# A third raw weight buffer, and all small weight parts on VectorE, in a hybrid decoder layer

## The chip, the cores and the metric

The kernel runs on one core of a Trainium2 chip. The metric is device time in microseconds (us) of one execution; the kernel before was timed three times. TensorE (PE) multiplies, VectorE (DVE), ScalarE (ACT) and GpSimd (POOL) work elementwise, and SyncE (SP) issues most transfers. SBUF is the memory on the core in which all operands stand; PSUM receives the products.

## The reference

One layer of a decoder for 256 tokens of width 1024, in float32. Cut to what matters:

```python
xn = rmsnorm(h, norm_mix_g[l])
q_a, k_a, v_a, q_b, f_b, i_b, og_b, g_a, g_b = split_cols(xn @ w_in[l])   # nine 1024-wide projections
y_a = moba_attention(q_a, k_a, v_a, positions) @ w_br_attn[l]             # rotary, causal softmax, 16 heads
y_b = hgrn2(q_b, f_b, i_b, og_b, lb_all[l], hgrn_norm_g[l]) @ w_br_hgrn[l] # gated linear recurrence, 8 heads
h = h + (sigmoid(g_a) * y_a + sigmoid(g_b) * y_b) @ w_out[l]
h = h + memory_cross_attention(rmsnorm(h, norm_x_g[l]), rmsnorm(mem, norm_mem_g[l]),
                               wq_x[l], wkv_x[l], wo_x[l])                # 4 heads, 256 memory tokens
gu = rmsnorm(h, norm_ffn_g[l]) @ w_ffn_in[l]
h = h + (silu(gu[..., :2816]) * gu[..., 2816:]) @ w_ffn_out[l]
return rmsnorm(h, final_norm_g)
```

With 256 tokens there is one attention block, so each query attends its own block alone.

## The kernel before, in words

**Weight chunks.** All weights are laid out beforehand as chunks of 128 x 2048 float32 (1 MB), in the order of `plan()`. The first 64 chunks, 0 to 63, belong to everything ahead of the feed-forward part: 0 to 3 the forget gate, 4 to 7 the recurrence's query, 8 to 27 the other projections, 28 to 35 the two merge gates, 36 to 47 the branch and output matrices, 48 to 63 the cross-attention. Chunk 60 to 63 are `wo_x`. For float32 accuracy each chunk is split into a large part `hi` (rounded by ScalarE, L210) and a small part `lo` = raw - hi (L214), and a product is made of three multiplications: hi by hi, hi by lo, lo by hi (L275 to L277).

**`prep()`** does one chunk: SyncE loads it into a raw buffer (L202, L204 or L208), ScalarE makes `hi` in two halves of 1024 columns, and VectorE makes `lo`. For chunks 9 to 41 (`SHARED`) each half of `lo` is divided: VectorE takes 576 columns and GpSimd 448 (`POOL_COLS` / 2). The raw buffers are two (pool `wr`), the buffers of `hi` and `lo` three each (`wh`, `wl`). Chunk 1 has a raw buffer of its own under the tag B14; chunks 62 and 63 have their parts (`hix`, `lox`) under the tags B10, B11 and B12, B6. `nxt()` hands the next chunk to a multiplication and first calls `prep()` for all chunks up to two ahead (`LEAD`), so when TensorE begins with chunk i, chunk i+2 may be split, into the buffer that chunk i-1 leaves.

**Order.** TensorE's instructions run in the order in which the code writes them. Side work (the recurrence `hgrn`, the attention `duo`, the scores of the cross-attention) is cut into steps that `tick()` runs between multiplications. For the other engines a planner, which has its own estimate of costs, orders the instructions; each engine, and SyncE's queue of transfers, then runs in that order, and an instruction that waits holds up all behind it on its engine. In the feed-forward part the order on all engines is written by hand.

**Big buffers.** `big(tag, ...)` gives buffers that are used again under their tag, each use waiting for the last readers of the one before. The ones that matter here: B0 holds `H`, the residual, which is loaded from the token-major input `xtok` at the start, squared for the first norm (L560, into `junk` under P1) and added to from L961 and L963 on. P0 holds `QK`, the recurrence's queries and keys. B6 is 16 KB a partition: first `QQ` (16 x 256 a partition; the moving operands of the pair products, L609 and L654), then in turn `oal`, `qxl`, `lox`, and in the feed-forward part `hids`, four slots of hidden activations.

**The cross-attention's end.** `scores(x)` makes the softmax of one head: the row maximum and product on VectorE (L1046), the exponential on ScalarE (L1050), the scaling on VectorE (L1054); TensorE then transposes it (L1060, tile `xT`) and `pv` multiplies it by the values (L270 to L272). Chunks 62 and 63 are prepared about there.

**Sums for the feed-forward part.** `block_sums()` adds pairs of weight chunks in device memory by accumulating transfers, issued by ScalarE (L228, L232) and GpSimd (L234) one by one as chunks are consumed.

Of the kernel before, what the change touches and what calls it, by code (L numbers as in the profile page):

```python
# [10 lines left out]
F32 = mybir.dt.float32  # L11
F32R = mybir.dt.float32r
I32 = mybir.dt.int32
AF = mybir.ActivationFunctionType
ALU = mybir.AluOpType
# [9 lines left out]
EPS = 1e-6  # L25
NEG = -1e30
LEAD = 2
POOL_COLS = 896
SHARED = range(9, 42)
TOKENS = ((0, 1), (1, 2), (2, 4), (4, 8))  # L30
WARM = 15
PIECES = (4, 2, 2)

D1, D2, D3, D4 = 6434.0, -0.01824188232421875, -3.5660341382026672e-06, 2.549093241608853e-10
C1, C2, C3 = 6.28125, 0.0019354820251464844, -1.748455600074497e-07
# [98 lines left out]
def build(tc, A, out):  # L134
    nc = tc.nc
    V, SC, G, PE, SY = nc.vector, nc.scalar, nc.gpsimd, nc.tensor, nc.sync
    with ExitStack() as ctx:
# [11 lines left out]
        def big(tag, name, shape=(128, 8, 256), dt=F32):  # L149
            return bp.tile(list(shape), dt, name=name, tag=tag)  # L150
# [21 lines left out]
        ifq, posi = gv[:, 56:88], gv[:, 88:90].bitcast(I32)  # L172
        nhalf = cp.tile([128, 4], F32, name="nhalf")
        ident = cst[:, C_ID:C_ID + 128]
        H = big("B0", "H", (128, 2, 1024))
        ones = cp.tile([128, 1], F32, name="ones")
        V.memset(nhalf, -0.5)
        V.memset(ones, 1.0)
# [5 lines left out]
        def prep(tags=None, raw=None):  # L184
            i = made[0]
            made[0] += 1
            first = i < 2
            if raw is None:
                raw = wr.tile([128, 2048], F32, name="raw", tag="raw")
            assert i in HEAD  # L190
            if tags is None:
                hi = wh.tile([128, 2048], F32R, name="hi", tag="hi")
                lo = wl.tile([128, 2048], F32R, name="lo", tag="lo")
            else:
                hi = big(tags[0], "hix", (128, 2048), F32R)
                lo = big(tags[1], "lox", (128, 2048), F32R)
            pieces = 4 if first else 2
            n = 2048 // pieces
            sent = PIECES[i] if i < len(PIECES) else 1
            for c in range(sent if 0 < i < len(PIECES) else 0):  # L200
                a = slice(c * 2048 // sent, (c + 1) * 2048 // sent)
                SY.dma_start(raw[:, a], piece(A["w"][i], a))  # L202
            if sent == 1:
                SY.dma_start(raw, A["w"][i])  # L204
            for c in range(pieces):
                a = slice(c * n, (c + 1) * n)
                if i == 0:
                    SY.dma_start(raw[:, a], piece(A["w"][i], a))  # L208
                    yield
                SC.activation(hi[:, a], raw[:, a], AF.Copy)  # L210
                cut = (c + 1) * n - (POOL_COLS // pieces if i in SHARED else 0)
                for eng, b in ((V, slice(c * n, cut)), (G, slice(cut, (c + 1) * n))):
                    if b.start < b.stop:
                        eng.tensor_tensor(lo[:, b], raw[:, b], hi[:, b].bitcast(F32), op=ALU.subtract)  # L214
            ready[i] = (hi, lo)

        def run(g):
# [83 lines left out]
        def gemm_t(X, evict, between=()):  # L301
            between = list(between)
            pss = [mm.tile([128, 512], F32, name="pst", tag="mm") for _ in range(2)]
            for kh in range(2):
                w = by_k(nxt(), 4)
                for t in range(2):
                    t_part(pss[t], w, X, t, kh)
                    if between:
                        between.pop(0)()
                    if kh == 1:  # L310
                        evict(t, pss[t])
                tick()
# [9 lines left out]
        def rstd_of(ssq, name, n=2, mult=1.0 / D, eps=EPS):  # L322
            v = small("v_", [n])
            V.tensor_scalar(v, ssq, mult, eps, op0=ALU.mult, op1=ALU.add)
            r = cp.tile([128, n], F32, name="r_" + name)
            G.tensor_tensor(r, v, nhalf[:, :n], op=ALU.pow)
            return r
# [142 lines left out]


        fT = big("B4", "fT", (128, 16, 128))
        QK = big("P0", "QK", (128, 2, 16, 128))
        QP, KS = QK[:, 0], QK[:, 1]
        QQ = big("B6", "QQ", (128, 16, 256))

        gate_a = cp.tile([128, 8], F32, name="gate_a")
        gate_b = cp.tile([128, 8], F32, name="gate_b")
# [38 lines left out]
        def ev_q(c):  # L517
            th = {}

            def use(h0, bk):  # L520
                a = slice(2 * h0, 2 * h0 + 4)
                q4 = bk.rearrange(v4, a=2)
                V.tensor_tensor(QP[:, a], q4, fT[:, a], op=ALU.mult)
                SC.activation(QQ[:, a].rearrange("p a (w j) -> p a w j", w=4)[:, :, 0:4:3],
                              q4.rearrange("p a (j w) -> p a w j", w=2), AF.Copy)

            def ev(t, ps):
                th[t] = t2("qth")
                SC.activation(th[t], ps, AF.Silu, scale=r_x[:, t:t + 1])
                if t == 1:  # L530
                    turned(th, c, use)
            return ev
# [4 lines left out]
        run(prep())  # L537
        SY.dma_start(cst, A["cst"])
        run(prep())
        SY.dma_start(H, A["xtok"])  # L540
        SY.dma_start(lm, A["lm"])
        pss = [[mm.tile([128, 512], F32, name="psg", tag="mm") for _ in range(2)] for _ in range(2)]
        for i in range(9):
            if i < 8:
                c, k = i // 4, i % 4
# [9 lines left out]
        for t in range(2):  # L555
            t_part(pss[0][t], w, X, t, 1)
        ssqx = small("ssqx", [2])
        junk = big("P1", "junk", (128, 2, 1024))
        for t in range(2):
            SC.activation(junk[:, t], H[:, t], AF.Square, accum_out=ssqx[:, t:t + 1])  # L560
        r_x = rstd_of(ssqx, "x")
        next(rt)
        next(rt)
        r_half = cp.tile([128, 2], F32, name="r_half")
# [39 lines left out]
        def level_one(g, bs):  # L604
            for b in bs:
                a0 = 8 * g + 2 * b
                ps = bank("l1", (128, 2, 64))
                for j in range(2):
                    PE.matmul(ps[:, j], KS[:, a0 + j], QQ[:, a0 + j, 0:64], start=True, stop=True)  # L609
                V.tensor_tensor(by_parity(a0, 0), ps, bc(ident2[:, :, 0], 2, 1), op=ALU.mult)  # L610

        def widen(g, L, parts="qkt"):
# [23 lines left out]
        def pair_queries(g, L):  # L636
            ga = slice(8 * g, 8 * g + 8)
            n = 32 // L
            mv = [QQ[:, ga, 64 * i:64 * i + 64] for i in range(3)]
            SC.activation(mv[0].rearrange("p a (i j) -> p a i j", j=L), blocks(QP[:, ga], L)[1], AF.Copy)  # L640
            widen(g, L, "qt")
            wide = blocks(QP[:, ga], 2 * L)[1]
            SC.activation(mv[1].rearrange("p a (i j) -> p a i j", j=2 * L), wide, AF.Copy)
            near = tview(L, g).rearrange("p a (i w) -> p a i w", w=4)[:, :, :, 1]
            V.tensor_tensor(mv[2].rearrange("p a (i j) -> p a i j", j=2 * L), wide,
                            near.unsqueeze(3).to_broadcast([128, 8, n, 2 * L]), op=ALU.mult)

        def pair_levels(g, L, bs):
            for b in bs:
                a0 = 8 * g + 2 * b  # L650
                n = 256 if L == 2 else 192
                ps = bank("lp", (128, 2, n))
                for j in range(2):
                    PE.matmul(ps[:, j], KS[:, a0 + j], QQ[:, a0 + j, 0:n], start=True, stop=True)  # L654
                if L == 2:
                    V.tensor_tensor(by_parity(a0, 1), ps[:, :, 192:256], bc(two_rows, 2, 1), op=ALU.mult)
                for i in range(3):
                    M = L if i == 0 else 2 * L
                    li = (1 if L == 2 else 4) + i
                    mask = lm[:, 64 * li:64 * li + 64].rearrange("p (i j) -> p i j", j=M)  # L660
                    V.copy_predicated(blocks(at3[:, a0:a0 + 2], M)[1], bc(mask, 2, 1),
                                      ps[:, :, 64 * i:64 * i + 64].rearrange("p a (i j) -> p a i j", j=M))
# [219 lines left out]
        def ev_g(dst, c):  # L882
            def ev(t, ps):
                SC.activation(dst[:, t, c * 512:(c + 1) * 512], ps, AF.Tanh, scale=r_half[:, t:t + 1])
            return ev
# [23 lines left out]
        turns = []  # L909
        for c in range(2):  # L910
            gemm_t(X, ev_g(tbt, c))
        tat = big("B7", "tat", (128, 2, 1024))
        for c in range(2):
            gemm_t(X, ev_g(tat, c))
# [275 lines left out]
        raws += spare + [big("B12", "raw", (128, 2048))]  # L1190
        fetch(4)
        fetch(5)
        hids = big("B6", "hids", (128, 4, 2, 2, 256), F32R)
        Sh = big("P1", "Sh", (128, 2, 4, 4, 128), F32R)
        ts = {}

# [40 lines left out]
        def turn_hid(o):  # L1237
            bk = four[1].rearrange("p (a b) -> p a b", a=2)
            for t in range(2):
                u = hm.pop((o, t))  # L1240
                for j in range(2):
                    PE.transpose(bk[:, j, t * 128:(t + 1) * 128], u[:, j * 128:(j + 1) * 128], ident)
            hd = hids[:, o % 4]
            hid[o] = hd

            def post():
                split(bk, hd[:, 0], hd[:, 1])
            return post
# [37 lines left out]
        for k, u in enumerate(FFN[:-2]):  # L1286
# [17 lines left out]
            w = use(k)  # L1304
# [155 lines left out]
```

## Time and profile before

| | |
|---|---|
| Time, median of 3 | 624.73 us (623.67 to 625.43) |
| The profiled execution's own time | 626.06 us |
| Its span, first to last instruction | 624.3 us |
| Busy: TensorE / VectorE / ScalarE / GpSimd | 606.2 / 450.5 / 369.2 / 210.2 us |
| Mean granted TensorE clock | 0.991 of full speed |

In the profile's rows `L214` is line 214 of the kernel, `lo<-raw,hi` the tiles written and read, `x66` the count, then the summed busy time in us and the mean of one in ns; behind it the engine's idle time ahead of these instructions and what ended it. In an answer in order of time the first two columns are the start and the length in us, and a bracket holds how long the engine had been idle and what released it. Rows of windows give start:end, the length, then for TensorE, its weight loads, VectorE, ScalarE and GpSimd the busy time with the count of instructions, then the granted clock, the share of time in which the DMA engines were busy, and GB/s. Rows of DMA issues end with KB and the median us from issue to landing.

### The profile page before, as it was taken

To read this page: it belongs to the slowest core of one execution; us is meant where nothing else is said; L and a number is where in the kernel's file an instruction comes from. 1 tells how busy PE (TensorE), PEld (TensorE's weight loads), DVE (VectorE), ACT (ScalarE), POOL (GpSimd) and SP (SyncE) were. 2 spreads that over 40 slices of the span, in tenths; PEclk is the share of its full clock that TensorE was granted. 3 is DMA by queue.
4 is the path that set the end of the run, shared out by engine and by line. 5 is a ranking of instruction groups with operands and counts; after the bars stand their busy time and mean duration, and the time that the engine had idled before them with its cause. 6 is when DMAs were issued, how large, how long until landed. Compare 5 with 4: busy or idle time off the path is not lost.

```text
span 624.3 us, 8396 instructions
## 1 busy us (share of the span) xinstructions
PE 606.2 (97%) x3075; PEld 503.1 (81%) x3075; DVE 450.5 (72%) x729; ACT 369.2 (59%) x583; POOL 210.2 (34%) x202
## 2 busy tenths in 40 slices
PE   8999999999999999999999999959999999999995
PEld 7888888888877887778888888858888888888884
DVE  7556678987776775747966557746789878787863
ACT  7775454334267666745546557555477767676752
POOL 3887844665464565343302433100000000000003
PEclk9999999999999999999999999979999999999998
DMA  9775898636875656797798887765699989896601
GB/s 342 289 276 210 266 318 262 228 140 198 270 208 204 257 152 198 276 322 265 228 286 240 304 283 239 229 256 203 264 289 356 307 333 288 319 319 227 195 1 67
DMA packets 21689, 154.70 MB, mean 248 GB/s; under 512 B 2720, under 2 KB 3360, under 8 KB 5280
## 3 DMA queue, kind: packets, MB, share of 16 engines
q1 hardware_dynamic: 17568, 116.63, 49.4%
q0 software_dynamic: 2880, 20.97, 17.4%
q10 hardware_dynamic: 1200, 16.57, 7.0%
q8 instruction: 24, 0.39, 0.2%
q14 instruction: 17, 0.14, 0.1%
HBM read 153.11 MB, written 32.51 MB: 297 GB/s over the span
## 4 chain that ended last, share of the span: by engine, by line
PE 78%; DMA 9%; DVE 8%; ACT 2%; issue 1%; POOL 0%; POOLq 0%; ACTq 0%; DVEq 0%; SPq 0%
PE pst L275 10%; PE pst L277 10%; PE pst L276 10%; DMA raw<-w 8%; PE bk L275 6%; PE bk L277 6%; PE bk L276 6%; DVE lo L214 4%; PE psf L290 3%; PE acc L275 3%; PE acc L277 3%; PE acc L276 3%; PE lp L654 2%; PE psf L291 2%; ACT hi L210 1%
## 5 line engine op out<-in xcount | busy, mean ns | idle before, releaser
L214 DVE TENSOR_TENSOR lo<-raw,hi 128x576 fp32r<-128x576 f32 (+2 forms) x128 | 143.7, 1137 | 68.4 <-ACT hi L210 67.4
L210 ACT ACTIVATE hi<-raw 128x1024 fp32r<-128x1024 f32 (+1 forms) x128 | 128.0, 1028 | 109.1 <-DMA raw<-w 53.6
L214 POOL TENSOR_TENSOR lo<-raw,hi 128x448 fp32r<-128x448 f32 x66 | 98.0, 1504 | 79.2 <-ACT hi L210 72.9
L275 PE MATMUL pst<-hi,Xh 128*128 128x512 f32 x256 | 103.2, 403 | 0.0
L277 PE MATMUL pst<-hi,Xl 128*128 128x512 f32 x256 | 99.9, 390 | 0.0
L276 PE MATMUL pst<-lo,Xh 128*128 128x512 f32 x256 | 99.7, 390 | 0.0
L1165 DVE TENSOR_TENSOR lo<-raw,hi 128x1024 fp32r<-128x1024 f32 x56 | 65.9, 1218 | 13.0 <-ACT hi L1164 12.8
L1164 ACT ACTIVATE hi<-raw 128x1024 fp32r<-128x1024 f32 x56 | 56.2, 1053 | 19.8 <-issue 10.5
L277 PEld LDWEIGHTS pst<-hi,Xl 128*128 128x128 f32 x256 | 48.0, 188 | 10.3
L275 PEld LDWEIGHTS pst<-hi,Xh 128*128 128x128 f32 x256 | 48.1, 188 | 10.0 <-issue 0.7
L276 PEld LDWEIGHTS pst<-lo,Xh 128*128 128x128 f32 x256 | 48.2, 188 | 9.2
L1147 POOL DMA_DIRECT2D raw<-w x5 | 4.5, 891 | 119.2 <-DVE lo L1165 29.7
L275 PE MATMUL acc<-hi,hids 128*128 128x512 f32 x64 | 25.1, 392 | 0.0
L277 PE MATMUL acc<-hi,hids 128*128 128x512 f32 x64 | 24.9, 390 | 0.0
L276 PE MATMUL acc<-lo,hids 128*128 128x512 f32 x64 | 24.9, 389 | 0.0
L275 PE MATMUL bk<-hi,Sh 128*128 128x512 f32 x60 | 23.7, 396 | 0.0
L275 PE MATMUL bk<-hi,h2h 128*128 128x512 f32 x60 | 23.7, 394 | 0.0
L277 PE MATMUL bk<-hi,h2l 128*128 128x512 f32 x60 | 23.4, 390 | 0.0
L277 PE MATMUL bk<-hi,Sh 128*128 128x512 f32 x60 | 23.4, 390 | 0.0
L276 PE MATMUL bk<-lo,h2h 128*128 128x512 f32 x60 | 23.4, 389 | 0.0
L276 PE MATMUL bk<-lo,Sh 128*128 128x512 f32 x60 | 23.3, 389 | 0.0
L290 PE MATMUL psf<-H,hi 128*128 128x512 f32 x64 | 22.8, 400 | 0.0
(388 smaller groups left out, 1446.8 us busy)
## 6 DMA issues: line engine op xcount, KB each, us to landing
raw<-w SPq DMA_DIRECT2D x78, 1024.0 KB, 6.4
sum<-w POOLq DMA_DIRECT2D x15, 1024.0 KB, 9.8
raw<-sum SPq DMA_DIRECT2D x13, 1024.0 KB, 6.9
raws<-w SPq DMA_DIRECT2D x11, 1024.0 KB, 6.7
raw<-w POOLq DMA_DIRECT2D x5, 1024.0 KB, 8.7
raw<-w SPq DMA_DIRECT2D x4, 512.0 KB, 6.1
raws<-sum SPq DMA_DIRECT2D x2, 1024.0 KB, 6.3
raw<-w SPq DMA_DIRECT2D x4, 256.0 KB, 4.5
```

What stands on the lines that cost most here:

```text
L210: SC.activation(hi[:, a], raw[:, a], AF.Copy)
L214: eng.tensor_tensor(lo[:, b], raw[:, b], hi[:, b].bitcast(F32), op=ALU.subtract)
L275: PE.matmul(ps, xh, h, start=first, stop=False, skip_group_check=more)
L276: PE.matmul(ps, xh, l, start=False, stop=False, skip_group_check=more)
L277: PE.matmul(ps, xl, h, start=False, stop=last, skip_group_check=more)
L290: PE.matmul(ps, w[0][:, k, a], X2[:, :, k], start=k == 0, stop=False)
L291: PE.matmul(ps[:, 0], w[1][:, k, a], X2[:, 0, k], start=False, stop=k == 7)
L654: PE.matmul(ps[:, j], KS[:, a0 + j], QQ[:, a0 + j, 0:n], start=True, stop=True)
L1147: G.dma_start(raw_of[k], A["w"][AT_CHUNK["I", PAIRS[g][0], 1]], accum_op=ALU.add)
L1164: SC.activation(hi[:, a], raw[:, a], AF.Copy)
L1165: V.tensor_tensor(lo[:, a], raw[:, a], hi[:, a].bitcast(F32), op=ALU.subtract)
```

## The change

Four edits. (1) `prep()` gives every third chunk (2, 5, 8, ...) a raw buffer outside the pool of two: under B0 for chunks below 32, under a new tag B6b from then on. (2) GpSimd's share of the small parts is gone; VectorE makes each half whole. (3) To free B0, the token-major input is loaded into P0 at the start as `xtok`, where it is squared in place, and loaded again into B0 as `H` behind the first merge gate's multiplications; `QK` is allocated under P0 behind the squares. (4) To have B6b, B6's 16 KB become two tags of 8 KB: `QQ` and `hids` are each a list of two halves.

```diff
-POOL_COLS = 896
-SHARED = range(9, 42)
+THIRD = 32
...
-        H = big("B0", "H", (128, 2, 1024))
...
-            if raw is None:
+            if raw is None and i % 3 == 2:
+                raw = big("B0" if i < THIRD else "B6b", "raw", (128, 2048))
+            elif raw is None:
                 raw = wr.tile([128, 2048], F32, name="raw", tag="raw")
...
                 SC.activation(hi[:, a], raw[:, a], AF.Copy)
-                cut = (c + 1) * n - (POOL_COLS // pieces if i in SHARED else 0)
-                for eng, b in ((V, slice(c * n, cut)), (G, slice(cut, (c + 1) * n))):
-                    if b.start < b.stop:
-                        eng.tensor_tensor(lo[:, b], raw[:, b], hi[:, b].bitcast(F32), op=ALU.subtract)
+                V.tensor_tensor(lo[:, a], raw[:, a], hi[:, a].bitcast(F32), op=ALU.subtract)
...
-        QK = big("P0", "QK", (128, 2, 16, 128))
-        QP, KS = QK[:, 0], QK[:, 1]
-        QQ = big("B6", "QQ", (128, 16, 256))
+        xtok = big("P0", "xtok", (128, 2, 1024))
+        QQ = [big(tag, "QQ", (128, 8, 256)) for tag in ("B6", "B6b")]
...
-        SY.dma_start(H, A["xtok"])
+        SY.dma_start(xtok, A["xtok"])
...
-        junk = big("P1", "junk", (128, 2, 1024))
         for t in range(2):
-            SC.activation(junk[:, t], H[:, t], AF.Square, accum_out=ssqx[:, t:t + 1])
+            SC.activation(xtok[:, t], xtok[:, t], AF.Square, accum_out=ssqx[:, t:t + 1])
         r_x = rstd_of(ssqx, "x")
+        QK = big("P0", "QK", (128, 2, 16, 128))
+        QP, KS = QK[:, 0], QK[:, 1]
...
-                    PE.matmul(ps[:, j], KS[:, a0 + j], QQ[:, a0 + j, 0:n], start=True, stop=True)
+                    PE.matmul(ps[:, j], KS[:, a0 + j], QQ[g][:, a0 + j - 8 * g, 0:n], start=True, stop=True)
...
             gemm_t(X, ev_g(tbt, c))
+        H = big("B0", "H", (128, 2, 1024))
+        SY.dma_start(H, A["xtok"])
         tat = big("B7", "tat", (128, 2, 1024))
...
-        hids = big("B6", "hids", (128, 4, 2, 2, 256), F32R)
+        hids = [big(tag, "hids", (128, 2, 2, 2, 256), F32R) for tag in ("B6", "B6b")]
...
-            hd = hids[:, o % 4]
+            hd = hids[o % 4 // 2][:, o % 2]
```

More of the change, by code (lines that the diff above doesn't have):

```diff
@@ L523, in use @@
                 V.tensor_tensor(QP[:, a], q4, fT[:, a], op=ALU.mult)
-                SC.activation(QQ[:, a].rearrange("p a (w j) -> p a w j", w=4)[:, :, 0:4:3],
+                qa = slice(a.start % 8, a.start % 8 + 4)
+                SC.activation(QQ[a.start // 8][:, qa].rearrange("p a (w j) -> p a w j", w=4)[:, :, 0:4:3],
                               q4.rearrange("p a (j w) -> p a w j", w=2), AF.Copy)
@@ L608, in level_one @@
                 for j in range(2):
-                    PE.matmul(ps[:, j], KS[:, a0 + j], QQ[:, a0 + j, 0:64], start=True, stop=True)
+                    PE.matmul(ps[:, j], KS[:, a0 + j], QQ[g][:, a0 + j - 8 * g, 0:64], start=True, stop=True)
                 V.tensor_tensor(by_parity(a0, 0), ps, bc(ident2[:, :, 0], 2, 1), op=ALU.mult)
@@ L638, in pair_queries @@
             n = 32 // L
-            mv = [QQ[:, ga, 64 * i:64 * i + 64] for i in range(3)]
+            mv = [QQ[g][:, :, 64 * i:64 * i + 64] for i in range(3)]
             SC.activation(mv[0].rearrange("p a (i j) -> p a i j", j=L), blocks(QP[:, ga], L)[1], AF.Copy)
```

## The prediction

> **What bounds the kernel now.** I read the page's engine table first, then who TensorE waited for, then the windows around those waits, then the instructions there.
>
> ```profile
> span 624.3 us, 8396 instructions
> PE 606.2 (97%) x3075; PEld 503.1 (81%) x3075; DVE 450.5 (72%) x729; ACT 369.2 (59%) x583; POOL 210.2 (34%) x202
> ```
>
> TensorE is busy for 606.2 of 624.3 us, and the change issues the same matmuls. So nothing can be won except in the 18 us in which TensorE stands still. Part of that is the start and the tail, where no weight chunk of the kind in question is awaited. The rest is in this answer on TensorE's waits (columns: sum, times, longest):
>
> ```profile
> PE xT L1060 <- DVE xp L1054: 6.3, 1, 6.3
> PE aT L829 <- DVE ap L821: 1.7, 3, 0.9
> PE xs L277 <- POOL qxl L1017: 0.8, 1, 0.8
> PE as L805 <- ACT pT L831: 0.5, 1, 0.5
> PE mT L903 <- POOL tat L898: 0.3, 1, 0.3
> ```
>
> Those five sum to 9.6 us. None of them is a wait for a weight part; all are for softmax or projection steps that travel through ScalarE and VectorE. The reader should ask what held these engines. The largest wait has a second cost, seen in the windows (start:end, then busy time per engine, granted clock, DMA share and GB/s):
>
> ```profile
> 110.00:115.00 5.00, 5.00 (x26) 4.36 (x25) 4.97 (x9) 2.64 (x3) 2.44 (x2) 1.00 0.00 0
> 410.00:415.00 5.00, 0.41 (x2) 0.33 (x3) 3.24 (x6) 4.10 (x8) 0.00 (x0) 0.67 0.23 95
> 415.00:420.00 5.00, 5.00 (x31) 5.00 (x31) 2.57 (x5) 2.24 (x4) 0.00 (x0) 0.65 0.90 344
> ```
>
> After the long gap the granted clock is 0.65 to 0.67; everywhere else in the body it is 1.00. The first row shows the other half of the story: from 110 to 115 us the DMA engines move nothing, because both raw buffers are full and wait to be split, and the transfer for the next chunk starts late.
>
> **Why the long wait exists.** On ScalarE, around it:
>
> ```profile
> 403.13 0.57 ACT L316 ACTIVATE ph<-xT 128x512 fp32r<-128x512 f32 x1
> 409.79 2.00 ACT L210 ACTIVATE hix<-raw 128x1024 fp32r<-128x1024 f32 x2 [6.08 <-DMA raw<-w]
> ```
>
> The large part of chunk 62 (tile hix) stands ahead of the last softmax's exponential in ScalarE's queue and waits 6.08 us for its transfer. Queued behind it are the exponentials, then VectorE's reciprocal and scaling, then TensorE's transpose xT. The transfer was late for want of a buffer:
>
> ```profile
> 391.28 0.33 SPq L204 DMA_DIRECT2D raw<-w  x1
> 399.91 0.33 SPq L204 DMA_DIRECT2D raw<-w  x1
> ```
> ```profile
> 389.99 1.22 DVE L214 TENSOR_TENSOR lo<-raw,hi 128x1024 fp32r<-128x1024 f32 x1
> 404.81 1.22 DVE L214 TENSOR_TENSOR lo<-raw,hi 128x1024 fp32r<-128x1024 f32 x1
> ```
> ```profile
> 399.91 9.79 DMA raw<-w
> 411.79 1.18 ACT xp L1050 x4
> ```
>
> Chunk 61's transfer left at 391.28, as VectorE finished chunk 59 (389.99 + 1.22 = 391.21). Chunk 62's left at 399.91, after chunk 60, and took 9.79 us.
>
> **Part 1: the third raw buffer.** After the change chunk 62 (62 % 3 = 2) uses the buffer that chunk 59 left. So it can leave at about 391.2 instead of 399.9, which is 8.7 us earlier, and with the same 9.79 us it lands at 401.0. ScalarE then starts hix right behind ph, at 403.13 + 0.57 = 403.7, and ends at 405.7 (2.00). The exponentials end 1.18 later, at 406.9. I assume that the planner keeps the order on both engines. On VectorE the second half of chunk 61 ends at 404.81 + 1.22 = 406.0; that one does not move, as its large part waits for TensorE to give back a weight buffer. Behind it come two halves of chunk 62 and the scaling:
>
> ```profile
> 413.07 1.20 DVE L214 TENSOR_TENSOR lox<-raw,hix 128x1024 fp32r<-128x1024 f32 x1
> 414.19 0.61 DVE L1054 TENSOR_SCALAR xp<-xp,xsum 128x256 f32<-128x256 f32 x2
> ```
> ```profile
> 407.88 0.39 PE L277 MATMUL pst<-hi,M 128*128 128x512 f32 x1
> 414.60 1.16 PE L1060 MATMUL xT<-cst,xp 128*128 128x128 f32 x4 [6.33 <-DVE xp L1054]
> 415.41 0.56 PE L270 MATMUL xo<-ph,vxh 128*128 128x256 f32 x1
> 418.53 0.28 PE L272 MATMUL xo<-ph,vxl 128*128 128x256 f32 x1
> 418.65 0.28 PE L270 MATMUL xo<-ph,vxh 128*128 128x256 f32 x1
> ```
>
> 406.0 + 2 x 1.20 + 0.61, with some 0.2 for the reciprocal, is 409.2. TensorE is ready at 407.88 + 0.39 = 408.3, so about 0.9 us of 6.33 stays: a gain of 5.4. With a gap of 0.9 us the clock should hold. The 14 matmuls from 415.41 to 418.53 took 3.12 us; at the later spacing (418.53 to 418.65, 0.12) they take 1.68: 1.4 us more. Bounds for this place: 0 (it stays whole) and 6.3 + 1.4 = 7.7 (exponential first).
>
> By the Trainium skill's page "TensorE: Matmul & The Clock Gate", section "HAM oscillation — how this bites in real kernels", the clock falls only after gaps above some 3.4 us. The two windows above agree for 6.33 us; by that rule the 1.4 us come back whenever less than 3.4 us remain, as summed.
>
> The three aT waits (1.7 us) have the same form:
>
> ```profile
> 179.40 2.01 ACT L210 ACTIVATE hi<-raw 128x1024 fp32r<-128x1024 f32 x2 [1.64 <-DMA raw<-w]
> 187.83 1.06 ACT L210 ACTIVATE hi<-raw 128x1024 fp32r<-128x1024 f32 x1 [3.24 <-DMA raw<-w]
> ```
>
> ScalarE stood 1.64 and 3.24 us for a transfer, in front of exponentials or copies that the transposes need. Each is longer than TensorE's own wait behind it (0.9 at most), and one buffer's lead is a whole chunk, so I take the full 1.7; bounds 0 and 1.7. The other waits (xs, as, mT: 1.6) go through GpSimd, a projection or a buffer held by the multiplication, and I leave them; bounds 0 and 1.6. What is late next is the raw buffer no longer but the large-part buffer, of which there are still three, given back by TensorE.
>
> **Part 2: all small parts on VectorE.** GpSimd loses 66 halves, VectorE's 66 grow from 576 to 1024 columns.
>
> ```profile
> L214 POOL TENSOR_TENSOR lo<-raw,hi 128x448 fp32r<-128x448 f32 x66 | 98.0, 1504 | 79.2 <-ACT hi L210 72.9 <-DVE lo L214 2.6 <-DVE ATS L656 1.9
> L214 DVE TENSOR_TENSOR lo<-raw,hi 128x576 fp32r<-128x576 f32 x66 | 69.3, 1059 | 33.2 <-ACT hi L210 32.6 <-issue 0.5
> L1165 DVE TENSOR_TENSOR lo<-raw,hi 128x1024 fp32r<-128x1024 f32 x56 | 65.9, 1218 | 13.0 <-ACT hi L1164 12.8
> L214 DVE TENSOR_TENSOR lo<-raw,hi 128x1024 fp32r<-128x1024 f32 x1 | 1.6, 1631 | 0.0
> L623 DVE TENSOR_TENSOR QK<-QK,Tt 128x512 f32<-128x512 f32 x10 | 12.2, 1220 | 0.0
> L623 DVE TENSOR_TENSOR QK<-QK,fT 128x512 f32<-128x512 f32 x2 | 1.4, 709 | 0.0
> ```
>
> A full half costs 1.218 us where GpSimd is quiet (the feed-forward row) and 1.631 in the one case in the busy stretch. Low bound: 66 x (1.218 - 1.059) = +10.5 us of VectorE. High bound: 66 x (1.631 - 1.059) = +37.8. I take the low one: the last two rows are the same operation, 1.220 us beside GpSimd and 0.709 away from it, so VectorE is being stretched by GpSimd now, and ten of these alone give back 5.1 us. Less work than 10.5 us net is spread over 240 us, and each small part is whole 1.2 us after its large part, not after GpSimd's 1.5. On TensorE's path: 0.
>
> The Trainium skill's page "SBUF — State Buffer", section "SBUF: two separate sides", says that a VectorE operation with two SBUF inputs and a GpSimd operation that reads SBUF exclude each other for the whole instruction. By that rule the relief is real, and with GpSimd's 98 us gone it is larger than the one group I summed.
>
> What hides the longer VectorE work is the lead of two chunks. Where that cover is thin, the stage rows say so:
>
> ```profile
> 95.00:137.00 42.00, 42.00 (x201) 35.86 (x200) 37.72 (x78) 16.29 (x20) 25.03 (x17) 1.00 0.66 226
> 180.00:262.00 82.00, 79.84 (x450) 62.31 (x449) 56.22 (x161) 56.98 (x127) 41.47 (x32) 1.00 0.67 218
> ```
> ```profile
> L214 DVE TENSOR_TENSOR lo<-raw,hi 128x576 fp32r<-128x576 f32 x13 | 14.0, 1081 | 0.0
> L214 DVE TENSOR_TENSOR lo<-raw,hi 128x576 fp32r<-128x576 f32 x21 | 20.4, 974 | 12.8 <-ACT hi L210 12.2 <-issue 0.5
> ```
>
> From 95 to 137 us VectorE is busy 37.72 of 42, with 13 halves (first group); from 180 to 262 it is 56.22 of 82, with 21 halves.
>
> **Part 3: input twice, buffers split.** The second load is one more transfer of 1 MB.
>
> ```profile
> H<-xtok SPq DMA_DIRECT2D x1, 1024.0 KB, 9.0
> ```
>
> It is issued past the middle of the projections, some 90 us before the residual sum reads it, in a stage with a DMA share of 0.67; it costs SyncE's queue one issue of 0.3 us. Cost 0; if its buffer were still held, the raw transfers behind it on that queue would wait, at most one 9.0 us landing, which two buffered chunks cover. At the opening, chunk 3 no longer waits for a buffer and chunk 4 may overtake the first load:
>
> ```profile
> 25.68 1.25 ACT L512 ACTIVATE fth<-psg,r_half 128x512 f32<-128x512 f32 x2
> 27.68 0.60 PE L490 MATMUL fT__411<-cst,fth 128*128 128x128 f32 x4
> ```
>
> The transposes at 27.68 need the first of these two activations, done at 26.3: a slack of 1.4 us. A chunk of 1 MB ahead of the load could cost as much as the load takes to land, 9.0 us, so the bounds are 0 and 7.6. I take 0, because chunk 3 is ahead of the load today too and would now leave earlier. The split query and hidden buffers issue the same instructions: 0.
>
> **Sum.** 5.4 + 1.4 + 1.7 = 8.5 us. The profiled execution took 626.06 us (624.3 of span and 1.8 around it), so 617.6 there. It lay 1.3 above the median of three, 624.73; against the median that is 616.2.
>
> **Rivals.** (a) *The long wait moves.* If the planner puts chunk 63's large part before the exponential too, ScalarE waits for that transfer, which leaves only after chunk 60 (399.9) and lands near 409.7 again. For it: the planner already misjudged this one. Against: program order has it later. Then only the 1.7 us remain: 623.0, or 621 where the transfer is quicker.
> (b) *VectorE becomes the bound.* If small parts cost 1.631, the stretch from 95 to 137 gets 13 x (1.631 - 1.081) = 7.2 us into 4.3 idle, so 2.9 come out. From 180 to 262, 21 x (1.631 - 0.974) = 13.8 us stand in the queue between the softmax steps, and the aT waits grow. All of it through, with the cross-attention gain of 6.8 kept, is 624.7 + 2.9 + 13.8 - 6.8 = 634.6. It decides once more than 6.8 of the 16.7 reach TensorE. Against: the 1.220 and 0.709 above.
> (c) *The third buffer buys nothing*, because large-part buffers gate the split anyway and the order on ScalarE puts other waits at the same places: 624.7. Against: 6.08 us of waiting was for the transfer, by name.
>
> **Numbers.** The forecast has 0.62, (a) 0.18, (b) 0.10, (c) 0.10. A measurement here can tell some 0.3%, 1.9 us. Faster: 0.62 and most of (a), 0.73; the same: the rest of (a) and nearly all of (c), 0.16; slower: (b) and a trace of (c), 0.11. Low end: all 9.6 us and the 1.4 gone, 613.7, less 0.7 of spread between runs: 613.0. High end: through (a) to (c), 624.5. The forecast's own range is 613.0 to 619.
>
> **What would show it.** Right: no wait of TensorE above 1.5 us at the last xT, no window below clock 1.00 near 410, no ScalarE wait of 6 us for a raw transfer, aT waits near 0, small parts at 1.22, the QK products near 0.71, DMA without empty windows up to 300 us, VectorE busy within 5 us of 450.5. Wrong: xT still late behind a transfer (a); small parts at 1.6 and new TensorE waits between 95 and 262 us (b); ScalarE's transfer waits gone but the span unmoved (c); TensorE idle at 27 us would be the opening.

## The result and the profile after

The changed kernel takes 614.42 us (median of 4, 614.12 to 615.0); the kernel before, on the same chip, 624.34 us (median of 4). The ratio is 0.9841 with a 95% interval of 0.9823 to 0.9858. The forecast was 616.2 us. The profiled execution went from 626.06 to 614.53 us, 11.5 us; against the median it is 9.9, as the profiled execution of before lay 1.7 above its median here.

The page of the changed kernel begins so (span, then busy time and share of each engine):

```profile
span 612.7 us, 8280 instructions
PE 603.5 (98%) x3075; PEld 501.3 (82%) x3075; DVE 445.3 (73%) x729; ACT 369.3 (60%) x583; POOL 116.9 (19%) x136
```

TensorE stands still for 612.7 - 603.5 = 9.2 us, where it was 18.1, and its busy time is 2.7 us less for the same matmuls. TensorE's waits, beside the start, show which standstills are left (sum, times, longest):

```profile
PE as L803 <- ACT pT L829: 0.5, 1, 0.5
PE mT L901 <- POOL tat L896: 0.2, 1, 0.2
PE xT L1060 <- DVE xp L1054: 0.2, 1, 0.2
```

The wait at xT is 0.2 us instead of 6.3, and aT and xs have left the list. To see what each place was worth altogether, and not only its named wait, take instructions that both traces have and look how far the changed kernel is ahead at each. From the timeline of TensorE, changed kernel:

```profile
174.72 1.03 PE L787 MATMUL rT<-cst,ra 128*128 128x128 f32 x8
298.48 0.49 PE L901 MATMUL mT<-cst,tat 128*128 128x128 f32 x3
374.82 0.28 PE L272 MATMUL xs<-kxh,qxh 128*128 128x256 f32 x1
376.14 0.28 PE L274 MATMUL xs<-kxh,qxl 128*128 128x256 f32 x1
404.50 0.81 PE L1060 MATMUL xT<-cst,xp 128*128 128x128 f32 x4 [0.21 <-DVE xp L1054]
419.29 0.38 PE L1110 MATMUL h2T<-cst,H 128*128 128x128 f32 x2
```

The same instructions in the kernel before (its xT row, 414.60, stands in the prediction):

```profile
174.84 1.03 PE L789 MATMUL rT<-cst,ra 128*128 128x128 f32 x8
301.20 0.49 PE L903 MATMUL mT<-cst,tat 128*128 128x128 f32 x3
377.58 0.28 PE L275 MATMUL xs<-kxh,qxh 128*128 128x256 f32 x1
380.06 0.28 PE L277 MATMUL xs<-kxh,qxl 128*128 128x256 f32 x1
430.80 0.38 PE L1110 MATMUL h2T<-cst,H 128*128 128x128 f32 x2
```

The leads are 0.12, 2.72, 2.76, 3.92, 10.10 and 11.51 us, and 11.6 at the end of the span. So 2.6 us were won between rT and mT, where the aT transposes lie; 1.2 inside one block of twelve xs matmuls; 6.2 up to the last xT; 1.4 behind it, in the stretch whose clock was 0.65; and next to nothing elsewhere.

The windows of the changed kernel that answer to those of before (granted clock third from the end, then DMA share and GB/s):

```profile
110.00:115.00 5.00, 5.00 (x26) 4.35 (x25) 5.00 (x11) 2.64 (x3) 0.83 (x1) 1.00 0.18 26
405.00:410.00 5.00, 5.00 (x44) 5.00 (x43) 3.83 (x5) 4.82 (x7) 0.00 (x0) 1.00 0.99 403
...
95.00:137.00 42.00, 42.00 (x200) 35.85 (x200) 35.84 (x78) 16.07 (x19) 7.67 (x6) 1.00 0.86 254
```

The clock stays at 1.00 behind the last softmax. From 95 to 137 us VectorE is busy 35.84 us where it was 37.72, although it now makes all small parts there.

Around the last softmax the order is what the prediction described, a little better. SyncE's queue, then VectorE, then ScalarE, changed kernel:

```profile
387.27 0.33 SPq L204 DMA_DIRECT2D raw<-w  x1
```
```profile
385.98 1.22 DVE L211 TENSOR_TENSOR lo<-raw,hi 128x1024 fp32r<-128x1024 f32 x1
...
399.96 1.22 DVE L211 TENSOR_TENSOR lo<-raw,hi 128x1024 fp32r<-128x1024 f32 x1
```
```profile
398.95 1.04 ACT L210 ACTIVATE hix<-raw 128x1024 fp32r<-128x1024 f32 x1
...
401.35 0.60 ACT L1050 ACTIVATE xp<-xp,xmx,r 128x256 f32<-128x256 f32 x1
405.15 2.01 ACT L210 ACTIVATE hix<-raw 128x1024 fp32r<-128x1024 f32 x2 [1.95 <-DMA raw<-w]
```

Chunk 62's transfer leaves at 387.27, as chunk 59's last small part ends (385.98 + 1.22 = 387.20). Its large part finds the data there: no wait in brackets at 398.95. Chunk 63's does wait for its transfer, 1.95 us at 405.15, but behind the exponentials, where nothing of TensorE's next work stands.

ScalarE's waits, before:

```profile
ACT hi L210 <- DMA raw<-w: 53.6, 21, 11.8
ACT hi L210 <- PE pst L277: 43.7, 16, 4.7
```

and after:

```profile
ACT hi L210 <- PE pst L274: 72.8, 23, 4.7
...
ACT hi L210 <- DMA raw<-w: 1.5, 2, 1.3
```

53.6 us of waiting for transfers became 1.5. Part of that time did not vanish: the wait for TensorE, which gives back the large-part buffers, grew by 29 us. It is the next limit of the supply. TensorE's own list names a large part once, for 0.2 us, so it costs TensorE next to nothing so far.

### The profile page after: what moved, and what is told of

Read it like the earlier page. It is cut to its first block, busy times and chain, and to the rows that moved or that the text cites. A ratio compares the mean times of both kernels' runs of the same rounds, so it can differ in the third digit from the quotient of the medians.

```text
span 612.7 us, 8280 instructions
## 1 busy us (share of the span) xinstructions
PE 603.5 (98%) x3075; PEld 501.3 (82%) x3075; DVE 445.3 (73%) x729; ACT 369.3 (60%) x583; POOL 116.9 (19%) x136
## 4 chain that ended last, share of the span: by engine, by line
PE 93%; DVE 4%; ACT 1%; issue 1%; DMA 1%; POOL 0%; POOLq 0%; DVEq 0%; ACTq 0%
PE pst L272 13%; PE pst L274 13%; PE pst L273 13%; PE bk L272 6%; PE bk L274 6%; PE bk L273 6%; PE psf L287 5%; PE acc L272 3%; PE acc L274 3%; PE acc L273 3%; PE psf L288 2%; PE lp L652 2%; DVE lo L211 1%; PE psg L545 1%; PE pso L274 1%; PE pso L272 1%
## 5 line engine op out<-in xcount | busy, mean ns | idle before, releaser
L211 DVE TENSOR_TENSOR lo<-raw,hi 128x1024 fp32r<-128x1024 f32 (+1 forms) x128 | 155.1, 1228 | 50.9 <-ACT hi L210 50.5
L231 POOL DMA_DIRECT2D sum<-w x15 | 13.0, 863 | 78.7 <-DMA sum<-sum 53.1
```

Of the source, the lines that this page charges most:

```text
L211: V.tensor_tensor(lo[:, a], raw[:, a], hi[:, a].bitcast(F32), op=ALU.subtract)
L231: tc.keep_in_program_order(G.dma_start(summed[g][i], A["w"][AT_CHUNK[u]], accum_op=ALU.add, max_dma_last_dim=8192))
```

## The experiments

The rival theories were these. **Buffer**: the third raw buffer is the cause of all that was won, and part 2 does nothing. **Order**: the long wait is not a want of a buffer but ScalarE's order, chunk 62's large part ahead of the exponentials. **VectorE**: the small parts' new place is worth something by itself. The kernels were timed in two groups, the first four and the last four, beside 17 and 23 executions of the kernel before, whose medians were 624.23 and 623.71 us. Ratios are against these.

**The buffer alone.** From the changed kernel, with GpSimd's share put back:

```diff
+POOL_COLS = 896
+SHARED = range(9, 42)
...
-                V.tensor_tensor(lo[:, a], raw[:, a], hi[:, a].bitcast(F32), op=ALU.subtract)
+                cut = (c + 1) * n - (POOL_COLS // pieces if i in SHARED else 0)
+                for eng, b in ((V, slice(c * n, cut)), (G, slice(cut, (c + 1) * n))):
+                    if b.start < b.stop:
+                        eng.tensor_tensor(lo[:, b], raw[:, b], hi[:, b].bitcast(F32), op=ALU.subtract)
```

> The changed kernel, but with GpSimd's share of the small parts of chunks 9 to 41 put back (448 of each 1024 columns). Theory (the third buffer makes the gain, by earlier transfers): 615 to 616.5 us; the wait of TensorE for xT is below 1 us and the granted clock at that place is full, as in the changed kernel; the aT waits are below 0.5 us; the QK products stay near 1.2 us and VectorE's busy time is some 5 us above the changed kernel's. Rival (freeing GpSimd makes a good part of it): 619 or more, with aT waits of 1.5 us or more.

Measured: 614.52 us (5 executions), ratio 0.9848 [0.9818, 0.9878], the time of the whole change and 0.5 below the range that was expected. The waits at aT and xs are gone and xT has 0.2 left. Two things differ from the changed kernel. The opening has a small wait of TensorE (tile fT, 0.5 us in two parts), and one group of ten QK products stays slow beside GpSimd's halves (VectorE's groups from 50 to 291 us):

```profile
L626 DVE TENSOR_TENSOR QK<-QK,Tt 128x512 f32<-128x512 f32 x10 | 11.8, 1184 | 0.0
```

VectorE is busy 451.3 us here and 445.3 in the changed kernel. So with the buffer there, part 2 frees VectorE by 6 us, and it is worth nothing in time that can be measured (614.52 against 614.42).

**VectorE alone.** From the kernel before, two buffers:

```diff
-                cut = (c + 1) * n - (POOL_COLS // pieces if i in SHARED else 0)
-                for eng, b in ((V, slice(c * n, cut)), (G, slice(cut, (c + 1) * n))):
-                    if b.start < b.stop:
-                        eng.tensor_tensor(lo[:, b], raw[:, b], hi[:, b].bitcast(F32), op=ALU.subtract)
+                V.tensor_tensor(lo[:, a], raw[:, a], hi[:, a].bitcast(F32), op=ALU.subtract)
```

> The kernel before, with only GpSimd's share of the small parts moved to VectorE. Theory: 622.5 to 624.5 us; the xT wait stays 5.5 to 7 us with a clock of about 0.65 behind it, because chunk 62's transfer still leaves only after chunk 60 is split; the QK products fall from 1.22 to about 0.72 us. Rival: 619 or less, as the softmax steps on VectorE come sooner and the aT, xs and xT waits shrink without a buffer.

Measured: 621.55 us (12 executions), ratio 0.9961 [0.9938, 0.9983]: 2.7 us won. That lies between what the theory (622.5 or more) and the rival (619 or less) had said, and each is half right. TensorE's waits, the window behind them and ScalarE at the last softmax:

```profile
PE xT L1057 <- DVE xp L1051: 5.6, 1, 5.6
```
```profile
410.00:415.00 5.00, 4.78 (x29) 4.71 (x30) 3.07 (x6) 1.86 (x3) 0.00 (x0) 0.67 0.77 315
```
```profile
405.41 2.00 ACT L210 ACTIVATE hix<-raw 128x1024 fp32r<-128x1024 f32 x2 [5.52 <-DMA raw<-w]
```

The long wait and its slow clock are still there, for the transfer. But the aT waits, which the prediction gave to the third buffer alone, are gone without it, and the xs wait with them. ScalarE's waits for transfers, 53.6 us before, are fewer:

```profile
ACT hi L210 <- DMA raw<-w: 33.2, 16, 8.1
```

So aT has two cures, each sufficient. How the second works is argued, not shown: a raw buffer is free once the last of its small parts is made, and with VectorE making all of it at 1.24 us a half that is earlier than with GpSimd's 1.50.

**A third buffer for chunk 62 alone.** From the kernel before:

```diff
-                run(prep(tags))
+                run(prep(tags, big("B4", "raw", (128, 2048)) if made[0] == 62 else None))
```

> The kernel before, with one raw buffer more for one chunk alone: chunk 62 is loaded into the buffer of the tag B4, free at that time. Theory (one late transfer ahead of the last softmax makes most of the loss): the xT wait falls from 6.3 to below 1.5 us, the clock stays full, the aT waits stay at 1.7 us; 616 to 618 us. Rival (the buffers must be three all along): above 620 us.

Measured: 616.7 us (6 executions), ratio 0.9883 [0.9857, 0.991]. TensorE's waits:

```profile
PE aT L829 <- DVE ap L821: 1.6, 3, 0.8
...
PE xT L1060 <- DVE xp L1054: 0.2, 1, 0.2
```

One chunk's buffer takes away the long wait and leaves aT. It is worth 7.5 us, where the whole change is worth 9.9.

**The order alone.** From the kernel before, with two buffers and GpSimd's share; the last softmax's exponentials and chunk 62's large part are held to the order of the program:

```diff
-                SC.activation(hi[:, a], raw[:, a], AF.Copy)
+                h = SC.activation(hi[:, a], raw[:, a], AF.Copy)
+                if i == 62:
+                    tc.keep_in_program_order(h)
...
-                SC.activation(p[:, t], p[:, t], AF.Exp, scale=one["r16"][:, t:t + 1], bias=mx[:, t:t + 1],
-                              accum_out=s[:, t:t + 1])
+                e = SC.activation(p[:, t], p[:, t], AF.Exp, scale=one["r16"][:, t:t + 1], bias=mx[:, t:t + 1],
+                                  accum_out=s[:, t:t + 1])
+                if x == 3:
+                    tc.keep_in_program_order(e)
```

> The kernel before with two raw buffers and GpSimd's share, but ScalarE's queue keeps the code's order for the last head's two exponentials and the large part of chunk 62, so that the exponentials come first. The transfer is as late as before. Theory (the loss is the order on ScalarE: work that is ready stands behind a load): the xT wait falls below 1.5 us, 616 to 618 us. Rival (the late transfer itself costs the time, whatever the order): TensorE then waits some 3 us or more for chunk 62 or 63 in the multiplication by wo, and the time is above 620 us.

Measured: 616.68 us (6 executions), ratio 0.9876 [0.9849, 0.9904], the same as with chunk 62's own buffer. TensorE's longest waits beside the start (xT is not in its list, xs has 0.5 left) and ScalarE's timeline:

```profile
PE aT L831 <- DVE ap L823: 1.7, 3, 1.0
```
```profile
404.19 0.60 ACT L1052 ACTIVATE xp<-xp,xmx,r 128x256 f32<-128x256 f32 x1 [1.28 <-DVE xmx L1050]
...
410.94 1.06 ACT L210 ACTIVATE hix<-raw 128x1024 fp32r<-128x1024 f32 x1 [0.76 <-DMA raw<-w]
```

The exponentials run at 404.19 and chunk 62's large part at 410.94, late for want of a buffer, and TensorE has no wait for it. So the late transfer cost time only because of the instruction that stood behind it: either an earlier transfer or another order takes the whole long wait away.

**The change without chunk 62's buffer.** From the changed kernel:

```diff
-            if raw is None and i % 3 == 2:
+            if raw is None and i % 3 == 2 and i != 62:
```

> The changed kernel, but chunk 62 is loaded into the pool of two again; every other third chunk keeps its own buffer. Theory (one late transfer makes most of the loss): the xT wait comes back at 5 to 6.5 us with the low clock behind it, and the time goes to 620.5 to 623 us. Rival (the gain is spread over the chunks): below 617 us.

Measured: 621.69 us (12 executions), ratio 0.997 [0.9949, 0.9991]. TensorE's waits:

```profile
PE xT L1060 <- DVE xp L1054: 5.2, 1, 5.2
```

This is the time of VectorE alone. All other third-buffer chunks together bring nothing measurable that part 2 doesn't bring already; chunk 62's brings 7.3 us. Here and in the kernel with one buffer for chunk 62, chunk 63's transfer moves as well, since the pool is then shared differently; that chunk 62's is the one that counts follows from the order run, in which neither transfer has a buffer more.

**Order and VectorE, two buffers.** The edits of the second and the fourth kernel together:

> The kernel before with two raw buffers, ScalarE's order kept for the last exponentials and the large part of chunk 62, and all small parts on VectorE. Theory: the two causes add, xT and aT waits are both gone, and the time equals the changed kernel's: 614 to 615.5 us, without a third buffer. Rival (the third buffer gives something of its own): 616.5 us or more.

Measured: 614.23 us (6 executions), ratio 0.9851 [0.9813, 0.9888]. No wait at aT, xs or xT; what stays is of this size (TensorE's waits):

```profile
PE psg L547 <- ACT hi L210: 0.6, 2, 0.3
PE as L804 <- ACT pT L830: 0.4, 1, 0.4
```

The whole gain is to be had without a third buffer, a second load of the input or a split of any buffer. It equals the changed kernel (614.42) within the spread. Beside the start, the waits left in either come to little over 1 us, so more of this kind has little left to win.

**What a gap costs by itself.** To measure the clock term, ScalarE copies the last softmax's scores onto themselves, two times or four, ahead of the exponentials; from the changed kernel:

```diff
+            for _ in range(2 if x == 3 else 0):
+                SC.activation(p, p, AF.Copy)
```

> The changed kernel with the last head's scores copied onto themselves twice on ScalarE ahead of the exponentials, which makes TensorE wait for xT on purpose. Expected: a wait of 1.5 to 2.5 us, the granted clock still full, so 616 to 617 us. If the clock falls after any gap above 1 us, 1.4 us more.

> As the run before with four copies, so that the wait for xT is 4 to 6 us. Expected: the clock falls to about 0.65 behind it, and the time is 620 to 622 us: the wait and some 1.4 us beside it. If only gaps above 6 us cost clock, the 1.4 us are missing.

Measured with two copies: 615.81 us (4 executions), ratio 0.9881 [0.9838, 0.9924], 1.4 above the changed kernel. The gap came out shorter than the 1.5 to 2.5 us that were meant. TensorE's wait and the window behind it:

```profile
PE xT L1062 <- DVE xp L1056: 1.1, 1, 1.1
```
```profile
405.00:410.00 5.00, 3.90 (x33) 3.82 (x33) 4.40 (x8) 4.35 (x6) 0.00 (x0) 1.00 0.99 395
```

Measured with four: 620.87 us (10 executions), ratio 0.9951 [0.9928, 0.9975], 6.5 above it. TensorE at the same places as in the result's section, and the window behind the gap:

```profile
175.35 1.03 PE L787 MATMUL rT<-cst,ra 128*128 128x128 f32 x8
409.64 0.83 PE L1062 MATMUL xT<-cst,xp 128*128 128x128 f32 x4 [4.75 <-DVE xp L1056]
425.64 0.60 PE L1112 MATMUL h2T<-cst,H 128*128 128x128 f32 x4
```
```profile
410.00:415.00 5.00, 5.00 (x31) 5.00 (x31) 2.85 (x4) 3.62 (x6) 0.00 (x0) 0.66 0.87 331
```

Against the changed kernel this execution is 0.63 us behind at rT, 5.14 at xT and 6.35 at h2T. So the opening cost 0.6, where the copies play no part and the cause is not shown; the gap cost 4.5, the 4.75 less the 0.21 that the changed kernel has there; and the matmuls behind the gap, in the window at 0.66, cost 1.2. With two copies the same three steps are 0.8, 0.9 and -0.3. So a gap of 1.1 us leaves the clock at 1.00 and costs about its length, and a gap of 4.75 is followed by a window at 0.66 and costs 1.2 more than its length. Both agree with the rule of the Trainium skill's page "TensorE: Matmul & The Clock Gate", section "HAM oscillation — how this bites in real kernels", whose threshold of some 3.4 us lies between them; no run here placed the threshold closer.

## Why the prediction was right, and where its sum was short

The direction, the mechanism at the last softmax and the range held. The sum was 8.5 us, and the leads add up to 11.6 on the same profiled executions. Term by term:

| place | said | found, by leads |
|---|---|---|
| opening, up to rT | 0 | 0.1 |
| aT stage, rT to mT | 1.7 | 2.6 |
| one block of xs | 0 | 1.2 |
| last xT | 5.4 | 6.2 |
| clock behind it | 1.4 | 1.4 |
| rest | 0 | 0.1 |

That the range held is in part luck. Its low end took 9.6 us of waits and 1.4 of clock, 11.0 together, for all that could be won, and on the profiled executions more than that was won. The medians differ by 9.9 only, because the profiled execution of before was one of its slower ones.

- **"I take the full 1.7"** for aT was too small by 0.9, because a wait's row counts only the standstill. Before, a run of six transposes broke in the middle:

```profile
193.14 0.55 PE L829 MATMUL aT<-cst,ap 128*128 128x128 f32 x3
194.18 0.70 PE L829 MATMUL aT<-cst,ap 128*128 128x128 f32 x3 [0.49 <-DVE ap L821]
```

after, it went through:

```profile
191.28 0.88 PE L827 MATMUL aT<-cst,ap 128*128 128x128 f32 x6
```

From 193.14 to 194.18 + 0.70 is 1.74 us, against 0.88: 0.86 for a wait of 0.49. The broken run of matmuls was itself longer, by the rest.
- **"I leave them"** for xs, as and mT was wrong for xs. The prediction counted its 0.8 as a matter of GpSimd; GpSimd waits there for ScalarE's rounding of the query, and just before it ScalarE, in the kernel before, had been held up by a large part that waited for TensorE, not for a transfer:

```profile
374.82 1.06 ACT L210 ACTIVATE hi<-raw 128x1024 fp32r<-128x1024 f32 x1 [3.23 <-PE psf L290]
```

  The wait is 0.5 with the order alone and not listed in the other kernels, that with a buffer for chunk 62 alone among them, though chunk 62's transfer comes only behind these matmuls. So the 1.2 need no third buffer for the chunks ahead; which part of the change brings them stays open.
- **"That one does not move"**, of chunk 61's second small part on VectorE, was the mis-sized step at xT. It moved from 404.81 to 399.96, 4.85 us, where the lead there was 3.92: 0.93 earlier than assumed, as the planner now has it ahead of the softmax's low part. That is most of the 0.9 said to remain, of which 0.2 did. The assumption that the planner keeps the order failed, in the harmless direction.
- **The clock term**, 1.4, came out as worked. The four-copy kernel gives 1.2 for a gap made on purpose.
- **Part 2 "on TensorE's path: 0"** holds beside the third buffer (614.52 against 614.42) and not without it: alone it wins 2.7 us. The same run shows that the aT waits, which the sum put down to the third buffer ("one buffer's lead is a whole chunk"), go with either part. The sum was right that they would go.
- **VectorE's balance** came out the other way. The two terms, +10.5 and -5.1, make 455.9, and within 5 us of 450.5 was to be the sign; it is 445.3, which is 5.2 below. The ten products were not all that got time back. VectorE's groups from 50 to 291 us, after:

```profile
L211 DVE TENSOR_TENSOR lo<-raw,hi 128x1024 fp32r<-128x1024 f32 x69 | 84.5, 1240 | 26.5 <-ACT hi L210 26.4
L621 DVE TENSOR_TENSOR QK<-QK,Tt 128x512 f32<-128x512 f32 x10 | 7.1, 713 | 0.0
```

The halves cost 1.240 (said 1.218) and the products 0.713 (said 0.709). Sixteen small operations of the attention softmax (tile anm) went from 525 to 162 ns each, which alone is 5.8 us.
- **The second load and the split buffers** cost nothing that shows, as said: the kernel of order and VectorE has neither and takes 614.23 us, against 614.42. At the opening a chunk did overtake the first load (transfers, ScalarE):

```profile
xtok<-xtok SPq DMA_DIRECT2D x1, 1024.0 KB, 11.9
```
```profile
25.54 1.85 ACT L508 ACTIVATE fth<-psg,r_half 128x512 f32<-128x512 f32 x3 [1.31 <-DVE r_half L563]
```
The load took 11.9 us instead of 9.0, and the activations that need it run together from 25.54. The third ends at 27.39, and TensorE's transposes start at 27.54 without a wait, so this cover is nearly used up.
- **The signs to watch** came out as listed but for two: VectorE's balance, above, and "DMA without empty windows". From 110 to 115 us the DMA share is still 0.18, at 26 GB/s. SyncE's queue still waits there for raw buffers (changed kernel, 95 to 137 us; 47.0 in the kernel before):

```profile
SPq L204 <- DVE lo L211: 30.9, 4, 9.7
```

  So three buffers fill up as two did. In the same stretch ScalarE waits 12.9 us for TensorE before it can make a large part, and until the parts are made a raw buffer is not free.

The rivals: (a) did not happen: chunk 63's large part did wait for its transfer, 1.95 us, but behind the exponentials, so it cost TensorE nothing. (b) is refuted by the 1.240 and the 35.84 above. (c) is refuted by chunk 62's buffer, 7.3 us in one direction and 7.5 in the other.

## What to carry to other kernels

A wait that ends at a transfer has two cures: bring the data earlier, or let nothing urgent stand behind the instruction that awaits it; the order can be the cheaper edit, as the order alone did here what the buffer did for the longest wait. When two parts of a change can each remove the same wait, the whole is less than their sum, and only runs of each part alone tell which are needed. Size a gain by the lead at instructions common to both traces, since wait rows leave out what a broken run of matmuls and a lowered clock cost.

## What the runs showed of the hardware

- **The clock falls some us after the last matmul, whether or not TensorE is back.** Windows of one microsecond, first the kernel before, then the one with four copies:

```profile
411.00:412.00 1.00, 0.00 (x0) 0.00 (x0) 1.00 (x1) 1.00 (x2) 0.00 (x0) 0.84 0.20 82
412.00:413.00 1.00, 0.00 (x0) 0.00 (x0) 0.11 (x2) 1.00 (x5) 0.00 (x0) 0.50 0.00 0
```
```profile
410.00:411.00 1.00, 1.00 (x7) 1.00 (x7) 1.00 (x1) 1.00 (x1) 0.00 (x0) 0.55 1.02 434
```

  In the kernel before the last matmul had ended at 407.88 + 0.39 = 408.27. The share of 0.84 is 1.00 up to 411.7 and 0.50 from there, so the clock halved 3.4 us later, in the middle of the gap, and was full again at 418.5, 6.8 us on. With four copies the last matmul ended at 404.90, the clock halved at 410.1, 5.2 us later, when the gap was already over, and was full again at 413.5. So neither the delay nor the length is fixed, and matmuls that run behind a gap can pay for it when the gap itself still shows 1.00.
- **VectorE beside GpSimd.** Ten products of 128x512 took 1.184 us each with GpSimd's halves in the same stretch and 0.713 without, the third buffer being there both times. With all that it got back, VectorE took over GpSimd's small parts at no cost in busy time: 450.5 us before, 445.3 after.
- **The spread went too.** The kernel before ran from 621.0 to 628.1 us over its 40 executions beside the experiments, the changed kernel from 614.1 to 615.0 over 4 and the kernel of order and VectorE from 613.8 to 614.9 over 6. In the kernel before the time goes with the mean granted clock: the five executions at 0.996 took 621.0 to 622.8 us, the six at 0.989 took 625.1 to 628.1. So part of the spread is how long the clock stayed low behind the long gap. That the gap itself varies because it ends at a transfer is argued, not shown.
